# Gating branch of a hybrid decoder layer: the weight of v's norm applied behind the spatial sum, and three scalings moved between engines

## The chip, the cores and the metric

The kernel runs on one core of one Trainium2 chip. Its engines work side by side, each through its own queue in order: TensorE (PE, matrix products; PEld is its loading of weights), VectorE (DVE), ScalarE (ACT), GpSimd (POOL) and SyncE (SP, which issues the DMAs). The metric is the device time of one execution in microseconds. Instructions wait for each other by semaphores; an instruction that waits holds up everything behind it on its engine.

## The reference

One layer with two groups of heads. The input projection of the normalised input gives u, v and a gate zg for group A, and x, B, C, z and dt for group B (a chunked state-space scan, called SSD here). Group A is what the change touches:

```
def spatial_gating(u, v, zg, v_norm_w, v_norm_b, ws, bs, out_norm_w):
    vn = layer_norm(v, v_norm_w, v_norm_b).reshape(bsz, nc, CHUNK, GMLP_HEADS, GMLP_HEAD_DIM)
    ws_c = jnp.where(causal[None], ws, 0.0)
    s = jnp.einsum('hts,bcshd->bcthd', ws_c, vn) + bs.T[None, None, :, :, None]
    y = u * s * jax.nn.silu(zg)
    return grouped_rms_norm(y, out_norm_w, GMLP_HEAD_DIM)
```

Chunks have 128 positions, there are 8 heads of 128 channels, 2048 positions and a model width of 1024, all in float32. The spatial sum runs over positions t and s; v's norm has its mean and its root per position, its weight and bias per channel. Both groups' outputs go through one output projection, a norm and the residual sum.

## The kernel before

The 2048 positions are worked on as four blocks b of four chunks of 128 (NT = 4). The projections are large products on TensorE in seven units of 28 steps: six units u = 0 to 5 for the input projection (u = 3 gives v, u = 4 and 5 give u and zg of two head pairs each), u = 6 for the output projection. Each float32 operand is split into two parts (lines 160 and 161, on ScalarE and VectorE), and three products per pair accumulate in `acc` (lines 165 to 167). Blocks are combined in pairs by a scheme with seven products per unit (P1 to P7); `after` (lines 870 to 906) empties the accumulators and combines them, partly on ScalarE (line 876), partly on VectorE (lines 890 to 906).

Beside these products run small tasks, generators that are advanced between steps by `run_tasks`, each `yield d` asking for a pause of d time units. The tile scheduler then sets each engine's order at build time from its own model of costs, so an edit in one task can move instructions of others. The tasks are: the SSD stream (lines 344 to 540: convolution in lines 370 and 372, decay factors E in lines 389 and 394, operands xdt, xde in lines 434 to 438, the chunk's products y_ps and st_ps in lines 448 to 453, state in lines 457 and 458, outputs in lines 460 to 465), and for each block b and head pair hp (16 times) the gate:

- `spatial` (line 574) loads four chunks of v, 128 positions by 256 channels; VectorE subtracts the mean and multiplies by v's norm weight (line 584), ScalarE multiplies by the root r per position (line 585); TensorE forms the spatial sums s_ps (line 594); VectorE adds SB, which holds the biases (line 598).
- `gate_in` (line 608), called as each chunk of u and zg comes out of the projection: VectorE multiplies y by u (line 613), ScalarE forms silu(zg) (line 615), GpSimd multiplies the two (line 616), ScalarE sums the squares of each head (line 184).
- `gate_out` (line 622) computes the root g_r over those sums (VectorE line 171, GpSimd line 173, a power), ScalarE multiplies each half of each chunk by it (line 627, eight instructions), and `y_tiles` has TensorE transpose y (line 553) and ScalarE empty the result with the norm's weight (line 555).

PSUM, where TensorE writes, has five buffers for `acc` and three for all small products, so a late eviction holds up TensorE. Tiles of 256 channels (v, y, sg, xdt, xde and others) share 22 buffers, and operands of the products 7 (`r`), whose loads wait for a buffer.

Of the kernel before, what the change touches and what calls it, by code (L numbers as in the profile page):

```python
# [10 lines left out]
AF = mybir.ActivationFunctionType  # L11
ALU = mybir.AluOpType
# [3 lines left out]
P = 128  # L16
# [35 lines left out]
def hybrid_kernel(ctx: ExitStack, tc: tile.TileContext, x, x_t, pre_w, w_u, w_o, w_dt,  # L52
                  v_w, v_b, ws_t, bs_t, gn_w, conv_w, conv_b, dt_bias, a_log, d_skip, sn_w,
                  post_w, out):
    nc = tc.nc
# [12 lines left out]
    def bank(name):  # L68
        return ps.tile([P, T], F32, name=name, tag="ps")
# [7 lines left out]
    def qt(name):  # L77
        return qpool.tile([P, GC], F32, name=name, tag="q")
# [37 lines left out]
    SB = const.tile([P, 8, P], F32, name="SB")  # L116
# [24 lines left out]
    row_w = {}  # L141
# [27 lines left out]
    def rsqrt_mean(ss, n, inv, name):  # L169
        ms = sm.tile([P, n], F32, name=name + "_ms")  # L170
        nc.vector.tensor_scalar(ms, ss, inv, EPS, ALU.mult, ALU.add)  # L171
        r = sm.tile([P, n], F32, name=name + "_r")
        nc.gpsimd.tensor_tensor(r, ms, mhalf[:, 0:n], ALU.pow)  # L173
        return r
# [372 lines left out]
    def y_tiles(b, yg, j):  # L547
        for i in range(2):
            if i:
                yield 0  # L550
            tp = bank("y_tp")
            for c in range(NT):
                nc.tensor.transpose(out=tp[:, c * P:(c + 1) * P], in_=yg[c][:, i * P:(i + 1) * P], identity=ident)  # L553
            yT = gt("yT")
            nc.scalar.activation(yT, tp, AF.Copy, scale=y_c[:, 2 * j + i:2 * j + i + 1])
            store(y_d[b][j][:, i, :], yT, lambda i=i: y_in.add((b, j, i)))
# [17 lines left out]
    def spatial(b, hp):  # L574
        cols = slice(hp * GC, (hp + 1) * GC)
        mv, r = v_mv[b]
        v = []
        for c in range(NT):
            vc = qt("v")
            nc.sync.dma_start(out=vc, in_=v_d[b][c, :, cols])  # L580
            v.append(vc)
        yield 6
        for vc, c in zip(v, range(NT)):
            nc.vector.scalar_tensor_tensor(vc, vc, mv[:, c, 0:1], row_w["v"][:, cols], ALU.subtract, ALU.mult)
            nc.scalar.activation(vc, vc, AF.Copy, scale=r[:, c:c + 1])
        yield 8
        yg = []
        for half in range(2):
            sps = bank("s_ps")
            for cc in range(2):  # L590
                c = 2 * half + cc
                for i in range(2):
                    h = 2 * hp + i
                    nc.tensor.matmul(sps[:, cc * 256 + i * P:cc * 256 + (i + 1) * P], lhsT=wsT[:, h, :],  # L594
                                     rhs=v[c][:, i * P:(i + 1) * P], start=True, stop=True)
            for cc in range(2):
                y = qt("y")
                nc.vector.tensor_tensor(y, sps[:, cc * 256:(cc + 1) * 256],
                                        SB[:, 2 * hp:2 * hp + 2, :].rearrange("p h d -> p (h d)"), ALU.add)
                yg.append(y)  # L600
            if half == 0:
                yield 0
        gate[b, hp] = yg
# [4 lines left out]
    def gate_in(b, hp, c, t):  # L608
        if c == 0:
            run_out(spatial_task[b, hp])  # L610
            g_ss[b, hp] = sm.tile([P, NT, 2], F32, name="g_ss")
        y, ss = gate[b, hp][c], g_ss[b, hp]
        nc.vector.tensor_tensor(y, y, t[:, 0:GC], ALU.mult)
        sg = qt("sg")
        nc.scalar.activation(sg, t[:, GC:2 * GC], AF.Silu)
        nc.gpsimd.tensor_tensor(y, y, sg, ALU.mult)
        for i in range(2):
            sumsq(ss[:, c, i:i + 1], y[:, i * P:(i + 1) * P], P)
        if c == NT - 1:
            spawn(gate_out(b, hp), 4)  # L620

    def gate_out(b, hp):
        yg, ss = gate[b, hp], g_ss[b, hp]
        r = rsqrt_mean(ss[:, :, :].rearrange("p c i -> p (c i)"), NT * 2, 1.0 / P, "g")
        for c in range(NT):
            for i in range(2):
                nc.scalar.activation(yg[c][:, i * P:(i + 1) * P], yg[c][:, i * P:(i + 1) * P], AF.Copy,
                                     scale=r[:, 2 * c + i:2 * c + i + 1])
        yield 14
        yield from y_tiles(b, yg, hp)  # L630

# [290 lines left out]
    for group in groups:  # L922
        i = group[0]
        u, p, name, j = steps[i][:4]
# [9 lines left out]
        for uu in (4, 5):  # L934
            for b, n, w in WANTED:
                if i == uu * 28 + w - 5:
                    spatial_task[b, 2 * (uu - 4) + n] = spawn(spatial(b, 2 * (uu - 4) + n), 1)
# [69 lines left out]
```

## Time and profile before

| | |
|---|---|
| median of 3 timed runs | 1588.07 us (1584.94 to 1588.9) |
| the profiled execution | 1584.35 us |
| its span, first to last instruction | 1582.57 us |
| mean granted TensorE clock | 0.979 |
| busy: PE, DVE, ACT, POOL | 1508.9, 1068.9, 819.8, 390.1 us |

The profile's page gives the busy time of each engine; the windows give the same for chosen stretches with the granted clock of TensorE (1.00 is full speed); the timeline lists instructions in order with the idle time in front of each and what ended it. A busy TensorE at full clock can't be helped by other engines; idle time of another engine costs nothing by itself.

### The profile page before, as it was taken

To read this page: it belongs to the slowest core of one execution; us is meant where nothing else is said; L and a number is where in the kernel's file an instruction comes from. 1 tells how busy PE (TensorE), PEld (TensorE's weight loads), DVE (VectorE), ACT (ScalarE), POOL (GpSimd) and SP (SyncE) were. 2 spreads that over 40 slices of the span, in tenths; PEclk is the share of its full clock that TensorE was granted. 3 is DMA by queue.
4 is the path that set the end of the run, shared out by engine and by line. 5 is a ranking of instruction groups with operands and counts; after the bars stand their busy time and mean duration, and the time that the engine had idled before them with its cause. 6 is when DMAs were issued, how large, how long until landed. Compare 5 with 4: busy or idle time off the path is not lost.

```text
span 1582.6 us, 21521 instructions
## 1 busy us (share of the span) xinstructions
PE 1508.9 (95%) x7268; PEld 1258.4 (80%) x7268; DVE 1068.9 (68%) x1708; ACT 819.8 (52%) x1769; POOL 390.1 (25%) x449
## 2 busy tenths in 40 slices
PE   4979999899999999999999999989999999999996
PEld 3868887788888888888778888867888878888775
DVE  3476874678665576567786768764665646587698
ACT  4432324655676545654466666859737742333332
POOL 1000000234232333342234515353523300000022
PEclk9988999999999999999999999989999999999999
DMA  9799999999998799986998788866776598897998
GB/s 333 264 371 357 338 411 397 392 340 366 374 349 311 240 353 341 329 316 238 333 338 319 271 299 275 279 229 225 276 252 242 193 302 326 275 384 239 341 351 333
DMA packets 160847, 494.63 MB, mean 313 GB/s; under 512 B 19040, under 2 KB 35808, under 8 KB 140768
## 3 DMA queue, kind: packets, MB, share of 16 engines
q1 hardware_dynamic: 160736, 493.25, 85.9%
q8 instruction: 57, 0.93, 0.2%
q14 instruction: 54, 0.44, 0.1%
HBM read 373.51 MB, written 119.67 MB: 312 GB/s over the span
## 4 chain that ended last, share of the span: by engine, by line
PE 57%; DMA 13%; DVE 11%; ACT 7%; issue 3%; POOL 1%; SPq 1%; DVEq 0%; ACTq 0%; POOLq 0%
PE acc L165 16%; PE acc L167 16%; PE acc L166 16%; DMA E<-scr 3%; DMA r<-yd 3%; PE y_ps L448 3%; ACT E L389 2%; DMA r<-w_o 2%; PE y_ps L451 1%; PE st_ps L453 1%; DVE cv_out L372 1%; DVE a L161 1%; PE s_ps L594 1%; PE y_tp L553 1%; DVE b L161 1%
## 5 line engine op out<-in xcount | busy, mean ns | idle before, releaser
L165 PE MATMUL acc<-b,a 128*128 128x512 f32 x1344 | 544.6, 406 | 16.1 <-DMA a<-as0P 5.4
L166 PE MATMUL acc<-b,a 128*128 128x512 f32 x1344 | 527.3, 392 | 0.0
L167 PE MATMUL acc<-b,a 128*128 128x512 f32 x1344 | 520.2, 393 | 4.3 <-DVE a L161 4.3
L165 PEld LDWEIGHTS acc<-b,a 128*128 128x128 f32 x1344 | 253.7, 189 | 71.3 <-DMA a<-as0P 5.6
L167 PEld LDWEIGHTS acc<-b,a 128*128 128x128 f32 x1344 | 253.2, 188 | 60.2 <-DVE a L161 6.3
L166 PEld LDWEIGHTS acc<-b,a 128*128 128x128 f32 x1344 | 254.0, 189 | 49.3
L160 ACT ACTIVATE a<-r 128x1024 fp32r<-128x1024 f32 x96 | 101.1, 1057 | 200.8 <-PE acc L167 88.5
L165 PE MATMUL acc<-a,b 128*128 128x512 f32 x448 | 182.4, 414 | 8.3 <-ACT b L160 4.2
L372 DVE SCALAR_TENSOR_TENSOR cv_out<-cv_raw,cw,cv_out 128x512 f32<-128x512 f32 x192 | 155.1, 810 | 41.5 <-ACT cv_out L370 39.5
L161 DVE TENSOR_TENSOR b<-r,b 128x1024 fp32r<-128x1024 f32 x112 | 141.9, 1270 | 60.6 <-ACT b L160 60.4
L166 PE MATMUL acc<-a,b 128*128 128x512 f32 x448 | 180.3, 403 | 0.8 <-DVE a L161 0.8
L167 PE MATMUL acc<-a,b 128*128 128x512 f32 x448 | 177.7, 400 | 0.0
L160 ACT ACTIVATE b<-r 128x1024 fp32r<-128x1024 f32 x112 | 117.2, 1052 | 86.9 <-PE acc L167 33.1
L161 DVE TENSOR_TENSOR a<-r,a 128x1024 fp32r<-128x1024 f32 x96 | 117.3, 1223 | 50.5 <-ACT a L160 50.3
L165 PEld LDWEIGHTS acc<-a,b 128*128 128x128 f32 x448 | 87.2, 195 | 27.4 <-ACT b L160 4.3
L184 ACT ACTIVATE junk<-y 128x128 bf16<-128x128 f32 (+1 forms) x192 | 65.5, 341 | 83.1 <-POOL y L465 71.4
L457 POOL TENSOR_TENSOR state<-state,ex 128x256 f32<-128x256 f32 x60 | 46.9, 781 | 239.5 <-PE y_ps L451 239.4
L166 PEld LDWEIGHTS acc<-a,b 128*128 128x128 f32 x448 | 86.8, 194 | 19.6 <-DVE a L161 1.8
L167 PEld LDWEIGHTS acc<-a,b 128*128 128x128 f32 x448 | 86.4, 193 | 18.9 <-issue 0.2
L436 POOL TENSOR_TENSOR xde<-xtok,dte 128x256 f32<-128x256 f32 x64 | 52.3, 824 | 165.0 <-ACT xtok L408 158.7
L173 POOL TENSOR_TENSOR o_r<-o_ms,mhalf 128x1 f32<-128x1 f32 x16 | 19.0, 1198 | 295.1 <-DVE o_ms L171 285.0
L389 ACT ACTIVATE E<-E,cs 128x128 f32<-128x128 f32 x256 | 79.6, 390 | 22.2 <-DMA E<-scr 22.2
(163 smaller groups left out, 2125.8 us busy)
## 6 DMA issues: line engine op xcount, KB each, us to landing
a<-as0P SPq DMA_DIRECT2D x64, 1024.0 KB, 7.4
a<-as1P SPq DMA_DIRECT2D x64, 1024.0 KB, 6.2
r<-w_u SPq DMA_DIRECT2D x108, 512.0 KB, 6.4
r<-yd SPq DMA_DIRECT2D x72, 512.0 KB, 5.3
r<-hd SPq DMA_DIRECT2D x48, 512.0 KB, 7.5
r<-w_o SPq DMA_DIRECT2D x36, 512.0 KB, 5.2
E<-scr SPq DMA_DIRECT2D x64, 256.0 KB, 7.4
yd<-yT SPq DMA_DIRECT2D x64, 256.0 KB, 4.4
```

The lines of the kernel that those rows point to most:

```text
L160: nc.scalar.activation(w[:, :, 0, :], t, AF.Copy)
L161: nc.vector.tensor_tensor(w[:, :, 1, :], t, w[:, :, 0, :], ALU.subtract)
L165: nc.tensor.matmul(dst, lhsT=a_hi, rhs=b_hi, start=first, stop=False, skip_group_check=True)
L166: nc.tensor.matmul(dst, lhsT=a_hi, rhs=b_lo, start=False, stop=False, skip_group_check=True)
L167: return nc.tensor.matmul(dst, lhsT=a_lo, rhs=b_hi, start=False, stop=last, skip_group_check=True)
L173: nc.gpsimd.tensor_tensor(r, ms, mhalf[:, 0:n], ALU.pow)
L184: nc.scalar.activation(junk[:, 0:n], src, AF.Square, accum_out=dst)
L372: nc.vector.scalar_tensor_tensor(cv, raw[:, j:j + T], cw[:, ti, j:j + 1], cv, ALU.mult, ALU.add)
L389: nc.scalar.activation(E[:, h, :], E[:, h, :], AF.Relu, scale=-1.0, bias=dts[self.b]["cs"][:, o + h:o + h + 1])
L436: nc.gpsimd.tensor_tensor(h4(xde[:, :]), xc, hv(d["dte"], g, c), ALU.mult)
L448: nc.tensor.matmul(yps[:, h * HD:(h + 1) * HD], lhsT=E[:, h, :], rhs=xdt[:, h * HD:(h + 1) * HD], start=True, stop=True)
L457: nc.gpsimd.tensor_tensor(h4(st[:, :]), h4(st[:, :]), ev(d["ex"], 1, g, c), ALU.mult)
```

## The change

By linearity, the weight of v's norm, which is per channel, can be applied behind the sum over positions. So VectorE's line 584 becomes a scalar operation with two per-position operands (mean and root), and ScalarE's scaling of v goes. Behind the spatial sum VectorE multiplies by the weight (line 598, where SB was added), and GpSimd adds SB (line 599, new). In `gate_out`, ScalarE's eight scalings per gate become four products of 128x256 on GpSimd, with g_r broadcast along each head (line 627). Between lines 586 and 597, and from 628 on, the changed kernel's line numbers are one less than before.

```
@@ -581,8 +581,7 @@
         for vc, c in zip(v, range(NT)):
-            nc.vector.scalar_tensor_tensor(vc, vc, mv[:, c, 0:1], row_w["v"][:, cols], ALU.subtract, ALU.mult)
-            nc.scalar.activation(vc, vc, AF.Copy, scale=r[:, c:c + 1])
+            nc.vector.tensor_scalar(vc, vc, mv[:, c, 0:1], r[:, c:c + 1], ALU.subtract, ALU.mult)
@@ -595,8 +594,9 @@
             for cc in range(2):
                 y = qt("y")
-                nc.vector.tensor_tensor(y, sps[:, cc * 256:(cc + 1) * 256],
-                                        SB[:, 2 * hp:2 * hp + 2, :].rearrange("p h d -> p (h d)"), ALU.add)
+
+                nc.vector.tensor_tensor(y, sps[:, cc * 256:(cc + 1) * 256], row_w["v"][:, cols], ALU.mult)
+                nc.gpsimd.tensor_tensor(y, y, SB[:, 2 * hp:2 * hp + 2, :].rearrange("p h d -> p (h d)"), ALU.add)
                 yg.append(y)
@@ -623,9 +623,8 @@
         for c in range(NT):
-            for i in range(2):
-                nc.scalar.activation(yg[c][:, i * P:(i + 1) * P], yg[c][:, i * P:(i + 1) * P], AF.Copy,
-                                     scale=r[:, 2 * c + i:2 * c + i + 1])
+            y = yg[c][:, :].rearrange("p (i d) -> p i d", i=2)
+            nc.gpsimd.tensor_tensor(y, y, r[:, 2 * c:2 * c + 2].unsqueeze(2).broadcast_to([P, 2, P]), ALU.mult)
```

The scheduler orders the engines anew from the first gates on. Three places show it. The first is ScalarE early in unit 5, between two groups of line 876 (875 in the changed kernel), which empty accumulators; E, xtok and btok belong to the SSD stream, sg, v, y and yT to the gates. Before:

```order
L555 ACTIVATE yT<-y_tp,y_c 128x512
L184 ACTIVATE junk,g_ss<-y 128x128
L585 ACTIVATE v<-v,v_r_7296 128x256 x4
L394 ACT_TABLE_LOAD
L394 ACTIVATE E<-E 128x512
L408 ACTIVATE xtok<-xt_tp 128x512
L394 ACTIVATE E<-E 128x512 x2
L184 ACTIVATE junk,s_ss<-y 128x256
L555 ACTIVATE yT<-y_tp,y_c 128x512
L615 ACT_TABLE_LOAD
L615 ACTIVATE sg<-acc 128x256
L627 ACTIVATE y<-y,g_r 128x128 x8
```

and in the changed kernel:

```order
L555 ACTIVATE yT<-y_tp,y_c 128x512
L615 ACT_TABLE_LOAD
L615 ACTIVATE sg<-acc 128x256
L471 ACTIVATE y<-y,s_r 128x256 x4
L394 ACT_TABLE_LOAD
L394 ACTIVATE E<-E 128x512 x2
L408 ACTIVATE xtok<-xt_tp 128x512
L394 ACTIVATE E<-E 128x512
L555 ACTIVATE yT<-y_tp,y_c 128x512
L184 ACTIVATE junk,g_ss<-y 128x128
L615 ACT_TABLE_LOAD
L615 ACTIVATE sg<-acc 128x256 x2
```

The four scalings of v (line 585) and the eight of y (line 627) are gone; the loads of function tables stand as before.

The second place is VectorE at the end of unit 4 and the start of unit 5, some 20 us earlier. Lines 815 and 814 are the same subtraction on a weight operand, which waits for its load (r<-w_u); u_8272 and u_8264 are the same tile. Before:

```order
L463 TENSOR_TENSOR yo<-y_ps,ex_1125 128x256
L815 TENSOR_TENSOR r<-r 128x1024
L598 TENSOR_TENSOR y<-s_ps,SB 128x256
L613 TENSOR_TENSOR y<-y,u_8272 128x256
L598 TENSOR_TENSOR y<-s_ps,SB 128x256
L434 TENSOR_TENSOR xdt<-xtok,dt_577 128x256
L613 TENSOR_TENSOR y<-y,u_8287 128x256
L460 TENSOR_TENSOR y<-y_ps,xtok 128x256
L458 TENSOR_TENSOR state_243<-state_243,st_ps 128x256
L171 TENSOR_SCALAR g_ms<-g_ss 128x8
L463 TENSOR_TENSOR yo<-y_ps,ex_1125 128x256
L598 TENSOR_TENSOR y<-s_ps,SB 128x256 x2
```

and in the changed kernel:

```order
L818 TENSOR_TENSOR r<-r 128x1024
L598 TENSOR_TENSOR y<-s_ps,row_w 128x256 x2
L434 TENSOR_TENSOR xdt<-xtok,dt_577 128x256
L613 TENSOR_TENSOR y<-y,u_8264 128x256
L613 TENSOR_TENSOR y<-y,u_8279 128x256
L460 TENSOR_TENSOR y<-y_ps,xtok 128x256
L171 TENSOR_SCALAR g_ms<-g_ss 128x8
L458 TENSOR_TENSOR state_243<-state_243,st_ps 128x256
L814 TENSOR_TENSOR r<-r 128x1024
L372 SCALAR_TENSOR_TENSOR cv_out<-cv_raw,cw,cv_out 128x512 x3
L463 TENSOR_TENSOR yo<-y_ps,ex_1125 128x256
L598 TENSOR_TENSOR y<-s_ps,row_w 128x256 x2
```

The subtraction that waits for its load has moved behind two spatial sums, xdt, two gate products and the state; behind it now stand three convolution steps.

The third place is GpSimd in the same stretch, from the last gate products of one gate (line 616) on. Before:

```order
L616 TENSOR_TENSOR y<-y,sg 128x256 x4
L457 TENSOR_TENSOR state_243<-state_243,ex_1125 128x256
L436 TENSOR_TENSOR xde<-xtok,dte_1128 128x256
L438 TENSOR_TENSOR xtok<-xtok,hvec 128x256
L173 TENSOR_TENSOR g_r<-g_ms,mhalf 128x8
L464 TENSOR_TENSOR y<-y,yo 128x256
L465 TENSOR_TENSOR y<-y,zs 128x256
L457 TENSOR_TENSOR state_243<-state_243,ex_1125 128x256
L616 TENSOR_TENSOR y<-y,sg 128x256 x3
L436 TENSOR_TENSOR xde<-xtok,dte_1128 128x256
```

and in the changed kernel:

```order
L616 TENSOR_TENSOR y<-y,sg 128x256 x3
L599 TENSOR_TENSOR y<-y,SB 128x256 x2
L436 TENSOR_TENSOR xde<-xtok,dte_1128 128x256
L457 TENSOR_TENSOR state_243<-state_243,ex_1125 128x256
L438 TENSOR_TENSOR xtok<-xtok,hvec 128x256
L173 TENSOR_TENSOR g_r<-g_ms,mhalf 128x8
L627 TENSOR_TENSOR y<-y,g_r 128x256 x4
L464 TENSOR_TENSOR y<-y,yo 128x256
L599 TENSOR_TENSOR y<-y,SB 128x256
L465 TENSOR_TENSOR y<-y,zs 128x256
L599 TENSOR_TENSOR y<-y,SB 128x256
L457 TENSOR_TENSOR state_243<-state_243,ex_1125 128x256
```

Behind g_r there are now the four products of line 627, and the third and fourth addition of a gate (line 599) stand behind those.

## Rows read from the trace of the kernel before

**Rows 1.** The page: busy us, share of the span, instructions.
```profile
PE 1508.9 (95%) x7268; PEld 1258.4 (80%) x7268; DVE 1068.9 (68%) x1708; ACT 819.8 (52%) x1769; POOL 390.1 (25%) x449
```

**Rows 2.** Windows: length, busy us (instructions) by engine, clock, DMA.
```profile
800.00:1300.00 500.00, 485.43 (x2477) 408.37 (x2476) 330.02 (x585) 334.86 (x895) 189.11 (x210) 0.99 0.77 268
...
1040.00:1060.00 20.00, 13.97 (x70) 11.15 (x68) 12.16 (x25) 13.50 (x48) 15.05 (x18) 0.90 0.82 288
1060.00:1080.00 20.00, 18.46 (x86) 15.72 (x87) 8.73 (x22) 16.60 (x46) 5.92 (x9) 0.76 0.33 102
1080.00:1100.00 20.00, 17.48 (x91) 14.06 (x90) 7.05 (x13) 19.70 (x53) 8.92 (x9) 1.00 0.67 228
...
1200.00:1220.00 20.00, 20.00 (x107) 16.98 (x106) 11.72 (x23) 14.48 (x52) 6.71 (x8) 1.00 0.73 254
```

**Rows 3.** Windows of 2 us, the same columns.
```profile
1050.00:1052.00 2.00, 2.00 (x11) 1.79 (x9) 0.83 (x3) 0.96 (x4) 1.91 (x3) 0.50 0.99 391
...
1058.00:1060.00 2.00, 0.00 (x0) 0.00 (x0) 2.00 (x3) 2.00 (x6) 1.61 (x3) 0.84 0.31 117
...
1062.00:1064.00 2.00, 2.00 (x8) 1.82 (x8) 1.46 (x3) 1.23 (x5) 0.00 (x0) 0.50 0.33 122
```

**Rows 4.** Timeline: start, us, engine, line, [idle before, releaser].
```profile
1045.44 1.22 DVE L815 TENSOR_TENSOR r<-r 128x1024 f32<-128x1024 f32 x1 [4.26 <-DMA r<-w_u]
...
1047.94 0.63 PE L553 MATMUL y_tp<-ident,y 128*128 128x128 f32 x4 [1.67 <-DVE y L598]
...
1051.04 2.44 ACT L627 ACTIVATE y<-y,g_r 128x128 f32<-128x128 f32 x8 [3.72 <-POOL g_r L173]
...
1053.96 0.80 ACT L370 ACTIVATE cv_out<-cv_raw,cb,cw 128x512 f32<-128x512 f32 x1
...
1054.80 1.54 DVE L372 SCALAR_TENSOR_TENSOR cv_out<-cv_raw,cw,cv_out 128x512 f32<-128x512 f32 x2 [1.63 <-ACT cv_out L370]
...
1060.55 0.41 DVE L434 TENSOR_TENSOR xdt<-xtok,dt 128x256 f32<-128x256 f32 x1
...
1061.02 1.97 PE L448 MATMUL y_ps<-xdt,E 128*128 128x64 f32 x8 [4.32 <-DVE xdt L434]
```

**Rows 5.** Timeline at 1097 us.
```profile
1097.14 1.55 ACT L876 ACTIVATE p<-acc 128x512 f32<-128x512 f32 x3
...
1097.77 0.50 PE L165 MATMUL acc<-b,a 128*128 128x512 f32 x1 [2.48 <-ACT p L876]
```

**Rows 6.** Lines of ScalarE, 810:1285: busy us, mean ns, idle before.
```profile
L627 ACT ACTIVATE y<-y,g_r 128x128 f32<-128x128 f32 x128 | 39.2, 392 | 18.7 <-POOL g_r L173 18.7
...
L585 ACT ACTIVATE v<-v,v_r 128x256 f32<-128x256 f32 x64 | 30.0, 501 | 21.8 <-DVE v L584 21.4
```

**Rows 7.** The same lines, 1067:1097.2.
```profile
L627 ACT ACTIVATE y<-y,g_r 128x128 f32<-128x128 f32 x8 | 2.4, 390 | 0.0
...
L585 ACT ACTIVATE v<-v,v_r 128x256 f32<-128x256 f32 x4 | 1.7, 504 | 0.0
```

**Rows 8.** Single lines: duration ns min/median/max, first and last start.
```profile
L584 DVE SCALAR_TENSOR_TENSOR v<-v,v_mv,row_w x64: 468/479/1059, 815.6 to 1229.0; 128x256 f32<-128x256 f32 x64
...
L138 DVE TENSOR_SCALAR SB<-SB,rsum,bsT x8: 342/343/344, 210.0 to 211.8; 128x128 f32<-128x128 f32 x8
...
L598 DVE TENSOR_TENSOR y<-s_ps,SB x64: 405/414/425, 843.4 to 1247.7; 128x256 f32<-128x256 f32 x64
...
L613 DVE TENSOR_TENSOR y<-y,c x16: 409/436/950, 955.7 to 1200.9; 128x256 f32<-128x256 f32 x16
...
L464 POOL TENSOR_TENSOR y<-y,yo x60: 719/742/1977, 320.0 to 1191.5; 128x256 f32<-128x256 f32 x60
...
L457 POOL TENSOR_TENSOR state<-state,ex x60: 604/614/1594, 318.0 to 1191.0; 128x256 f32<-128x256 f32 x60
...
L173 POOL TENSOR_TENSOR g_r<-g_ms,mhalf x16: 1635/1637/2095, 874.5 to 1262.2; 128x8 f32<-128x8 f32 x16
```

**Rows 9.** Waits, 810:1285: total us, times, longest.
```profile
POOL y L616 <- ACT sg L615: 67.9, 17, 9.6
```

## The prediction, made before the changed kernel ran

> **What bounds the kernel now.** First the busy shares: TensorE is busy for 95% of the span and ScalarE for 52% [rows 1]. An average like this hides where the time can still move, so the stretches come next, and only the one that the change can reach: the spatial products and gates run from about 810 to 1270 us. In 1200:1220 TensorE is busy for all 20 us at full clock [rows 2]. There nothing that other engines do can shorten the time. Over 800:1300 TensorE is busy for 485.43 of 500 us [rows 2], so 14.57 us of idle time is the most that can go there, apart from the clock. Three neighbouring stretches hold most of it: 20 − 13.97 = 6.03, 20 − 18.46 = 1.54 and 20 − 17.48 = 2.52 us, together 10.09 us in 1040:1100 [rows 2]. The other 4.48 us I take as unchanged. In the same place the granted clock is 0.90 and 0.76 [rows 2], and the finer stretches show that it stands at 0.50 (1.2 instead of 2.4 GHz) around 1050 and again from 1060 on, after TensorE had stood still for all of 1058:1060 [rows 3]. 20 × 0.10 + 20 × 0.24 = 6.8 us is the upper bound of what that clock cost, since part of it fell into idle time.
>
> So there are two places. **The pile at 1045 to 1070**: VectorE stands 4.26 us before the weight operand of line 815, which a DMA brings at 1045.44. ScalarE stands 3.72 us before the eight scalings of line 627, because GpSimd still computes g_r, and so starts the convolution's first step (line 370) at 1053.96, for which VectorE waits 1.63 us. VectorE reaches xdt (line 434) at 1060.55, and TensorE has waited 4.32 us for it when it starts at 1061.02 [rows 4]. **The end at 1097.77**: TensorE waits 2.48 us for ScalarE to empty an accumulator (line 876) [rows 5]. ScalarE was busy for 19.70 of 20 us before [rows 2], and had not waited.
>
> **The change part by part.** No DMA and no matmul is added or taken away; three engines change.
>
> *ScalarE* loses 64 scalings of v (30.0 us) and 128 of y (39.2 us) [rows 6]. Nearly all of that lies beside a busy TensorE and is worth nothing. What counts is the run between two groups of line 876: in 1067 to 1097 four scalings of v (1.7 us) and eight of y (2.4 us) stand in the full ScalarE [rows 7], and the new order has neither between those groups. Line 876 then comes 4.1 us earlier against a wait of 2.48 us, so that wait goes: **−2.5 us**. What is late next there is the split of b (line 160) or TensorE's own y_tp, which ends just before. Bounds 0 and −2.5.
>
> *VectorE*: line 598 reads another constant and stays at 0.414 us. Line 584 becomes a scalar operation with two per-partition operands. The trace has no such operation at this size: the nearest row below is line 138, the same operation on half the elements (0.343), the nearest above the old line 584 (0.479) [rows 8]. I take the upper one, 0.48, since I need no gain from it; both ends differ by 64 × 0.14 = 9 us of VectorE's time, beside TensorE. What moves matters more. The order puts line 814 (the old 815, which waits for the DMA) behind two of line 598, xdt, two gate products, 460, g_ms and 458; these now run in the 4.26 us in which VectorE stood. From the start of the DMA-bound instruction to the xdt that held TensorE it took 1060.55 − 1045.44 = 15.1 us [rows 4]. In the new order there stand between the two: line 814 (1.22), six of line 372 at 1.54 / 2 = 0.77, two of 598 and one 458 and 463 at 0.42, two of 613 at 0.43, four of 584 at 0.48 [rows 4, 8]: 1.22 + 4.62 + 1.68 + 0.86 + 1.92 = 10.3 us. The wait for line 370 goes too, because its ScalarE queue no longer waits for g_r. Xdt comes 4.8 us earlier, less 0.3 us for the new wait below: **−4.5 us**. The DMA's landing I leave where it is. TensorE still stops here for several us, so I credit nothing for the clock. Bounds: 0, if the DMA lands later by what is gained, and −14.4 us, all idle time of 1040:1080 (7.57) and all of the clock (6.8).
>
> *GpSimd* gains 64 additions and 64 products with a broadcast operand. The nearest rows are line 464, two full operands, 0.742 us, and line 457, one of them broadcast, 0.614 us [rows 8]: 64 × 0.742 + 64 × 0.614 = 87 us on top of 189 in 500 [rows 2], 276, or 55%. As an engine it does not become the bound. But the additions stand inside a chain: VectorE's gate product (line 613) now waits for GpSimd's line 599, and whatever stands behind 613 on VectorE, evictions of accumulators and splits of b among them, waits with it, and TensorE for those. Mostly six to sixteen VectorE instructions stand between 598 and 613, 2.5 us or more at 0.42, which covers 0.742. In the pile it is two or three: about 0.3 us each for three pairs, the first already counted. Line 627 now stands on GpSimd behind g_r: four of 0.614 = 2.5 us, against 2.4 on ScalarE, ahead of transposes that are issued 14 time units later; that costs nothing while GpSimd is free.
>
> *Collisions.* Line 584 goes from 0.468 to 1.059 us and line 613 from 0.409 to 0.950, line 457 from 0.604 to 1.594 [rows 8], while the two engines run side by side. Between 0 and 0.54 us for each of 128 new operations is 0 to 69 us of VectorE's time, on 330 of 500 [rows 2]. At the upper end it is 80% busy and still beside TensorE, except where TensorE waits for VectorE. I take **+1.0 us** for collisions and the new wait together; 0 and +5 are the bounds, the upper from the 4.26 us that a VectorE standing still cost in the pile.
> The Trainium skill, SBUF — State Buffer, "Who interferes with whom", says that VectorE and GpSimd share a port pair as an exclusive lock, which a VectorE instruction takes with two SBUF inputs, or as a tensor_scalar in its two-port mode; the second one blocks fully. By it the new line 584 can still collide, as the old one could. The spreads above agree with a block of about a whole instruction. With one full block per new operation the +1.0 would be about +2, and the time 1583.
>
> The sum: −2.5 − 4.5 + 1.0 = −6.0 us on the profiled execution's own 1584.35 us (1582.57 of span and 1.78 around it) = 1578.3. The median of the timed runs, 1588.07, is 3.72 us above that execution, so the forecast in its terms is **1582 us**, with a range of its own of 1577 to 1587 us.
>
> **Rivals.**
> *The pile closes.* With g_r's wait gone from ScalarE and the DMA's wait filled, TensorE keeps its clock: 7.57 + 6.8 + 2.5 − 1.0 = 15.9 less about 1.5 for clock loss that was idle: 14.4 us, **1573.7 us**. For it: the 1.67 us that TensorE waits at 1047 hang on a line 598 that now comes before the DMA wait [rows 4]. Against: by my own count xdt still comes at about 1056, long after TensorE wants it. Chance 0.14.
> *Hidden.* The DMA-bound instruction only waits in another place, and behind it stand the convolutions and 463, so the pile moves as a whole. Then −2.5 + 1.0 = −1.5: **1586.6 us**. For it: TensorE's wait at 1061 is at the end of one queue that starts with a DMA. Chance 0.14.
> *GpSimd's queue becomes the wait* (the other side). In the pile the third addition (599) stands behind g_r (1.637), four of line 627 (2.46) and one 464 (0.742): with its own 0.742 that is 5.6 us from g_ms [rows 8]. It decides from the point at which VectorE needs less than 5.6 us from g_ms to its third gate product; my count of what lies there (0.42 + 1.22 + 2.3 + 0.42 + 0.8 = 5.2 us) is close to that. GpSimd also stands in order before late ScalarE results, 67.9 us in 17 waits, up to 9.6 us [rows 9], and additions now queue behind these. One stop of VectorE of 5.6 us that reaches TensorE where it had none, with a clock loss of the size seen here (I take 5.5 us of the 6.8), against the 2.5 won: +8.6, **1596.7 us**. Against: the order interleaves the additions, and most pairs are far apart. Chance 0.24.
>
> **How the numbers follow.** The forecast has a chance of 0.48. About 0.3%, or 4.8 us, is what a measurement here tells from no change: 1583.3 and 1592.8 are the limits. Two thirds of the forecast lie under 1583.3 (0.32), the rest (0.16) is no change. Faster: 0.32 + 0.14 = 0.46; no change: 0.16 + 0.14 = 0.30; slower: 0.24. The range of 8 in 10 reaches from the better part of the closing pile to the middle of the slow case: 1572 to 1596 us.
>
> **What would show it.** Right: TensorE's wait for line 875 (the old 876) near 1095 is gone; ScalarE's busy time falls by about 69 us and GpSimd's rises by 87 to 110; the wait of y_ps for xdt ends some 4 to 5 us earlier; 1200:1220 is still full. Wrong: VectorE's line 613 waits for GpSimd's 599 by several us at a time and TensorE behind it; a stretch of half clock outside 1050 to 1070; or the old wait of 4.3 us is still there at full length.

## The result and the profile after

The changed kernel took 1597.34 us (median of 20 runs, 1589.7 to 1603.69), the kernel before 1587.9 us (20 runs beside it). The ratio on record is 1.0053 with a 95% interval of 1.0038 to 1.0067 (the two medians alone would give 1.0059): slower, by more than the 0.3% that can be told apart. The forecast of 1582 us had the wrong sign, and 1597.34 lies 1.3 us outside the range of 8 in 10 (1572 to 1596 us). The rival of GpSimd's queue had given 1596.7 us.

The span of the profiled execution grew from 1582.6 to 1593.1 us. The busy shares on the page of the changed kernel, which answer to [rows 1]:

```profile
PE 1506.3 (95%) x7268; PEld 1254.3 (79%) x7268; DVE 1089.3 (68%) x1708; ACT 759.0 (48%) x1577; POOL 492.2 (31%) x577
```

ScalarE has 61 us less and GpSimd 102 us more, close to the forecast (69 less, 87 to 110 more). VectorE has 20 us more with the same number of instructions. The windows, with the columns of [rows 2]:

```profile
800.00:1300.00 500.00, 474.95 (x2431) 397.47 (x2430) 344.83 (x580) 270.54 (x700) 290.48 (x339) 0.99 0.76 260
...
980.00:1000.00 20.00, 19.15 (x92) 15.89 (x92) 16.68 (x30) 14.24 (x46) 12.84 (x14) 0.91 0.73 246
...
1040.00:1060.00 20.00, 16.14 (x87) 12.81 (x85) 15.35 (x25) 7.95 (x26) 18.48 (x21) 1.00 0.77 282
1060.00:1080.00 20.00, 10.92 (x53) 9.48 (x54) 11.48 (x22) 10.79 (x38) 14.37 (x19) 0.74 0.39 134
1080.00:1100.00 20.00, 16.95 (x87) 13.44 (x86) 8.22 (x14) 18.33 (x46) 8.01 (x11) 1.00 0.52 179
1200.00:1220.00 20.00, 20.00 (x102) 17.05 (x102) 14.40 (x26) 8.90 (x30) 17.96 (x22) 1.00 0.60 216
```

In 800:1300 TensorE is idle for 25.05 us, before for 14.57 [rows 2]. The difference of 10.5 us is as large as the difference of the spans (1593.1 − 1582.6), and the two executions part here: the first spatial sum (line 598) starts 0.5 us later than before (843.9 against 843.4), the last one 11.4 us later (1259.1 against 1247.7; [rows 8] and the last section). 1200:1220 is still full. Of the 10.5 us, 5.4 lie in 1040:1080 (12.94 us idle instead of 7.57), where GpSimd is busy for 18.48 and 14.37 of 20 us, and 0.5 in 1080:1100. The remaining 4.6 us (9.06 idle instead of 4.48) are in stops of under 2 us each between 860 and 1160 us. Behind one of them the granted clock falls far from the pile, to 0.91 over 980:1000; that was one of the prediction's signs of being wrong. The timeline of the pile, in the columns of [rows 4]:

```profile
1044.89 1.75 DVE L818 TENSOR_TENSOR r<-r 128x1024 f32<-128x1024 f32 x1
1048.63 0.43 DVE L598 TENSOR_TENSOR y<-s_ps,row_w 128x256 f32<-128x256 f32 x1 [2.00 <-POOL y L616]
...
1052.83 0.24 DVE L171 TENSOR_SCALAR g_ms<-g_ss 128x8 f32<-128x8 f32 x1
...
1053.41 1.28 DVE L814 TENSOR_TENSOR r<-r 128x1024 f32<-128x1024 f32 x1
...
1053.58 2.62 POOL L173 TENSOR_TENSOR g_r<-g_ms,mhalf 128x8 f32<-128x8 f32 x1
1056.28 2.84 POOL L627 TENSOR_TENSOR y<-y,g_r 128x256 f32<-128x256 f32 x4
1059.08 0.72 POOL L464 TENSOR_TENSOR y<-y,yo 128x256 f32<-128x256 f32 x1
1059.77 0.72 POOL L599 TENSOR_TENSOR y<-y,SB 128x256 f32<-128x256 f32 x1
...
1060.52 0.93 DVE L613 TENSOR_TENSOR y<-y,u 128x256 f32<-128x256 f32 x1 [2.58 <-POOL y L599]
...
1067.79 0.41 DVE L434 TENSOR_TENSOR xdt<-xtok,dt 128x256 f32<-128x256 f32 x1
1068.35 1.94 PE L448 MATMUL y_ps<-xdt,E 128*128 128x64 f32 x8 [8.56 <-DVE xdt L434]
1071.54 0.99 PE L165 MATMUL acc<-b,a 128*128 128x512 f32 x1
...
1061.15 0.47 SPq L735 DMA_DIRECT2D a<-as1P  x1
```

Read it from the bottom up. TensorE stands 8.56 us for xdt, where it stood 4.32 before [rows 4]. VectorE comes to xdt 14.4 us after line 814 (1067.79 − 1053.41), not 10.3. In between, its gate product (line 613) waits 2.58 us for the addition (line 599), and the addition stands behind g_r, four products of line 627 and one line 464. Line 814 no longer waits for its DMA, but only because it starts at 1053.41 instead of 1045.44: ahead of it VectorE has waited for GpSimd again, for a buffer that line 616 frees (2.00 us).

The last row (SPq is the queue that issues SyncE's DMAs) shows a second wait that ends at almost the same moment. The accumulation at 1071.54 needs operand a, whose load (a<-as1P) is issued at 1061.15 and lands at 1067.96. Before, the same load was issued at 1047.08, right behind the load of w_u; now it stands behind the load of w_u that waits for line 814 (issued at 1054.72) and behind the loads of v, one of which waits 2.6 us for GpSimd's line 464 to free a buffer. So an earlier xdt alone would have let that accumulation start at 1067.96 at the earliest, 3.6 us sooner than it did.

The stop near 1097 us [rows 5] has changed. TensorE's two waits there in the changed kernel:

```profile
1094.04 1.16 PE L422 MATMUL cb_ps<-cv_out 128*128 128x128 f32 x8 [2.21 <-ACT xtok L408]
...
1097.12 0.50 PE L165 MATMUL acc<-b,a 128*128 128x512 f32 x1 [0.80 <-ACT sg L615]
...
PE acc L165 <- ACT p L875: 2.4, 2, 1.6
```

The wait for line 876 (now 875) is gone there, but others of ScalarE stand in its place: 1080:1100 has 3.05 us of idle time, before 2.52. Elsewhere it has come up anew: the last row has TensorE's waits for line 875 in 800:1300 (total us, times, longest), 1.63 us at 874 us and 0.74 at 1076, together 2.4 us, about as much as the one wait before.

### The profile page after: what moved, and what is told of

Its sections match the earlier page's. It is cut to its first block, busy times and chain, and to the rows that moved or that the text cites. A ratio compares the mean times of both kernels' runs of the same rounds, so it can differ in the third digit from the quotient of the medians.

```text
span 1593.1 us, 21479 instructions
## 1 busy us (share of the span) xinstructions
PE 1506.3 (95%) x7268; PEld 1254.3 (79%) x7268; DVE 1089.3 (68%) x1708; ACT 759.0 (48%) x1577; POOL 492.2 (31%) x577
## 4 chain that ended last, share of the span: by engine, by line
PE 58%; DMA 13%; DVE 11%; ACT 6%; issue 3%; POOL 1%; SPq 0%; DVEq 0%; ACTq 0%; POOLq 0%
PE acc L165 16%; PE acc L167 16%; PE acc L166 16%; DMA E<-scr 3%; PE y_ps L448 3%; DMA r<-yd 3%; DMA r<-w_o 2%; ACT E L389 2%; DVE a L161 2%; PE y_ps L451 1%; PE st_ps L453 1%; DVE cv_out L372 1%; DVE b L161 1%; PE y_tp L553 1%; PE s_ps L593 1%
## 5 line engine op out<-in xcount | busy, mean ns | idle before, releaser
L165 PE MATMUL acc<-a,b 128*128 128x512 f32 x448 | 182.1, 413 | 10.5 <-ACT b L160 4.7
L372 DVE SCALAR_TENSOR_TENSOR cv_out<-cv_raw,cw,cv_out 128x512 f32<-128x512 f32 x192 | 159.8, 835 | 35.8 <-ACT cv_out L370 33.0
L161 DVE TENSOR_TENSOR b<-r,b 128x1024 fp32r<-128x1024 f32 x112 | 145.1, 1298 | 49.4 <-ACT b L160 49.3
L376 ACT ACTIVATE cv_out<-cv_out 128x512 f32<-128x512 f32 x64 | 40.3, 630 | 109.5 <-DVE cv_out L372 109.1
```

The costliest lines, as they stand in the source:

```text
L161: nc.vector.tensor_tensor(w[:, :, 1, :], t, w[:, :, 0, :], ALU.subtract)
L165: nc.tensor.matmul(dst, lhsT=a_hi, rhs=b_hi, start=first, stop=False, skip_group_check=True)
L372: nc.vector.scalar_tensor_tensor(cv, raw[:, j:j + T], cw[:, ti, j:j + 1], cv, ALU.mult, ALU.add)
L376: nc.scalar.activation(self.cv[i], self.cv[i], AF.Silu)
```

## The experiments

All ratios are to the kernel before, with 95% intervals. My first theory after the result was the **block theory**: an addition that stands behind g_r and the four products of line 627 in GpSimd's queue stops VectorE's gate product. Its rivals were the chain (the addition alone), the load with its collisions, the buffers that GpSimd frees late, and the order of the instructions itself.

### Halves of the change

The scaling of y back on ScalarE (x1_y_act), and both that and the addition of SB on VectorE (x4_no_pool). Short diffs against the changed kernel:

```
-            y = yg[c][:, :].rearrange("p (i d) -> p i d", i=2)
-            nc.gpsimd.tensor_tensor(y, y, r[...].broadcast_to([P, 2, P]), ALU.mult)
+            for i in range(2):
+                nc.scalar.activation(yg[c][:, i * P:(i + 1) * P], ..., AF.Copy, scale=r[...])
x4_no_pool, also:
-                nc.gpsimd.tensor_tensor(y, y, SB[...], ALU.add)
+                nc.vector.tensor_tensor(y, y, SB[...], ALU.add)
```

> The changed kernel with the scaling of y (line 627) back on ScalarE; only the addition of SB stays on GpSimd. GpSimd then has some 46 us more than before instead of 102. Queue theory (GpSimd's queue is full in the dense stretch, mostly by the block of four products behind g_r): most of the 10 us goes, time 1588 to 1591 us (ratio to before 1.000 to 1.002), VectorE's wait for line 599 near 1060 under 1 us. Chain theory (the addition on GpSimd between lines 598 and 613 costs, wherever it stands): the loss stays, 1595 to 1599 (1.005). Chance order (any reordering of this place moves the time by this much): no forecast, anything from 1580 to 1600.

> The changed kernel with nothing added to GpSimd: the addition of SB on VectorE, the scaling of y on ScalarE; left of the change are line 584 with both scalars and the 64 scalings less on ScalarE (30 us), for 26 us more on VectorE. Queue theory and chain theory: both causes are gone, 1583 to 1588 (ratio 0.997 to 1.000). If VectorE itself is what the pile waits for (its own work, not GpSimd), 26 us more there show as a longer wait for xdt: 1592 or more.

x2_add_dve makes only the second edit; x3_y_pool_only puts line 627's new form into the kernel before and nothing else.

> The changed kernel with the addition of SB on VectorE behind line 598; the scaling of y stays on GpSimd as one product per chunk. VectorE gets 64 x 0.41 = 26 us more, GpSimd 50 us less. Queue theory: the four products behind g_r still block GpSimd, so that lines 464 and 616 and the buffers they free come late; half of the loss or more stays, 1592 to 1596 (ratio 1.002 to 1.005). Chain theory: the loss goes, 1584 to 1589.

> The kernel before with one edit, the scaling of y on GpSimd as one product per chunk (64 products instead of 128 scalings on ScalarE). Queue theory: this edit alone loses, 1592 to 1597 us (ratio 1.003 to 1.006), TensorE's wait for xdt grows. Chain theory: no addition in the chain, so no loss: 1583 to 1588 (0.997 to 1.000).

Measured: x1 1.0012 (0.9994 to 1.0030), x2 0.9992 (0.9975 to 1.0009), x3 0.9980 (0.9962 to 0.9998), x4 1.0000 (0.9985 to 1.0015). None has the loss of 0.5%. The chain theory, by which x1 should have kept it, fails; the queue theory in its first form, by which x2 and x3 should have kept half, fails too. VectorE as the bound fails with x2 and x4: x2 has VectorE busy for 361.92 us of 800:1300, more than the changed kernel (344.83), and loses nothing. So far only the two GpSimd parts together lose; the last part of this section tries that at other settings.

x2 also shows the second wait of the pile by itself. Its timeline:

```profile
1052.34 1.21 DVE L814 TENSOR_TENSOR r<-r 128x1024 f32<-128x1024 f32 x1
...
1045.76 0.39 SPq L735 DMA_DIRECT2D a<-as0P  x1
1053.58 0.33 SPq L153 DMA_DIRECT2D r<-w_u  x1
...
1055.83 0.38 SPq L735 DMA_DIRECT2D a<-as1P  x1
...
1063.41 0.79 PE L165 MATMUL acc<-b,a 128*128 128x512 f32 x1 [6.35 <-DMA a<-as1P]
1063.75 0.94 DVE L434 TENSOR_TENSOR xdt<-xtok,dt 128x256 f32<-128x256 f32 x1
1066.14 1.80 PE L448 MATMUL y_ps<-xdt,E 128*128 128x64 f32 x8
```

Here the xdt of the pile starts at 1063.75, 4.0 us earlier than in the changed kernel and 3.2 us later than before [rows 4], and TensorE doesn't wait for it. Yet 1040:1080 has 8.89 us of idle time (before 7.57, changed 12.94): TensorE first waits 6.35 us for its operand a. That DMA is issued at 1055.83, because SyncE's queue stood from 1045.76 to 1053.58 before the load of w_u, which went out when line 814 had ended. So beside the wait for xdt there is a second one, in SyncE's queue, that an earlier xdt alone doesn't remove.

### Block, buffers, load

The block cut in two with 13 units behind it (y1_split_block), ScalarE for the sixth and seventh gate alone (y2_two_gates), 25 buffers (y3_q25), and the load without the chain on the kernel before (y4_idle_load):

```
y1:          for c in range(NT):
+                if c == 2:
+                    yield 1
...
-        yield 14
+        yield 13
y2:  for gates 6 and 7 of 16 the ScalarE loop of x1
y3:  -  qpool ... bufs=22        +  qpool ... bufs=25
y4:  (before) +  nc.gpsimd.tensor_tensor(idle, SB[0:2], SB[2:4], ALU.add)   # behind 598, and 4 per gate
```

> The changed kernel with the block of four products of line 627 cut in two: one time unit between the second and the third, and 13 in place of 14 behind them, so that an addition (line 599), line 464 or line 616 can stand between. GpSimd's work is the same. Block theory (an addition that stands behind g_r and four products in GpSimd's queue stops VectorE's gate product, and neither does so alone): half of the loss or more goes, 1588 to 1593 us (ratio 1.001 to 1.003). Load theory (the sum of GpSimd's work and its collisions with VectorE costs, in whatever order): the loss stays, 1595 to 1599 (1.005).

> The changed kernel with the scaling of y back on ScalarE for two of the sixteen gates only, the sixth and the seventh, which are those of the pile at 1036 and 1056 us; GpSimd loses 8 products of 64 (5 us of its 102 more). Block theory: the 5.4 us more that TensorE stands in 1040 to 1080 go, 1590 to 1593 us (ratio 1.002 to 1.003). Load theory: a twentieth of the load goes, so 1596 to 1597 (1.005).

> The changed kernel with 25 buffers of the size of a gate's chunk instead of 22; no operation changes its engine. Buffer theory (VectorE's line 598 and ScalarE's silu wait for GpSimd only because it frees their buffers late, 6.0 us in six and 15.0 us in three waits): half of the loss or more goes, 1589 to 1593 us (ratio 1.001 to 1.003). Block theory, by the chain from 599 to 613: the loss stays, 1594 to 1598.

> The kernel before with 128 additions put on GpSimd at the places of the new ones (64 behind line 598, four in each gate behind g_r), which read a constant and write a tile that nobody reads: the same load, queue and collisions, without the chain from 598 over 599 to 613, and with ScalarE as full as before. Load theory: 1594 us or more (ratio 1.004 or more). Block theory: the chain is missing, so at most late buffers: 1587 to 1591 (1.000 to 1.002).

Measured: y1 1.0001 (0.9985 to 1.0018), y2 1.0011 (1.0000 to 1.0022), y3 1.0056 (1.0037 to 1.0076), y4 1.0212 (1.0191 to 1.0234). y1 has GpSimd as full as the changed kernel (289.45 us of 800:1300) and loses nothing, against the load theory; y2 puts an eighth of the products back and loses a fifth as much. By their times both fit the block theory. But the waits don't. In y2 the 5.4 us in 1040:1080 should have gone; TensorE is idle there for 10.81 us, only 2.1 less than in the changed kernel, and most of what y2 wins lies behind 1080. The load of a is issued as late there (1062.00) as in the changed kernel; y1 issues it at 1050.66. VectorE's waits for GpSimd in 800:1300 (total us, times, longest) of y1:

```profile
DVE state L458 <- POOL state L457: 9.4, 6, 2.8
DVE y L613 <- POOL y L599: 8.9, 7, 3.8
DVE y L598 <- POOL y L616: 2.2, 3, 1.3
```

of y2, TensorE's longest:

```profile
PE y_ps L448 <- DVE xdt L434: 6.5, 1, 6.5
```

and of y3, with TensorE's longest below:

```profile
DVE state L458 <- POOL state L457: 11.1, 9, 1.8
DVE y L598 <- POOL y L616: 0.3, 1, 0.3
...
PE acc L165 <- ACT sg L615: 5.2, 3, 2.5
PE y_ps L451 <- DVE state L458: 4.6, 3, 2.4
PE y_tp L553 <- ACT xtok L408: 4.4, 1, 4.4
```

y1 waits 8.9 us for the addition and loses nothing. y3 never waits for it, its waits for buffers are all but gone, and it loses 0.56%, in other places. So neither that wait nor late buffers can be the cause by themselves, and the block theory as one named stop has fallen.

y4 missed its aim. Its additions need no operand of the dense stretch, and all were run early:

```profile
210.17 3.23 POOL L601 TENSOR_TENSOR idle<-SB 128x256 f32<-128x256 f32 x4 [52.30 <-DVE SB L138]
...
341.69 6.33 POOL L631 TENSOR_TENSOR idle<-SB 128x256 f32<-128x256 f32 x8
...
PE y_ps L451 <- DVE state L458: 21.4, 1, 21.4
```

From 210 to 348 us they fill GpSimd; TensorE then waits 21.4 us for a state that comes behind them. It says nothing of the dense stretch, so the load without the chain remains untested there, but it shows that work which no one waits for costs 2% where it stands in front of work that someone does.

### The order itself

If the places of the loss change with each edit, the order of the instructions may be the cause. The number of time units between the scaling of y and its transposes (14) shifts the order and changes no operation:

```
-        yield 14
+        yield 13   (z1 changed kernel, z3 before)    15 (z2, z4)    16 (w1, v4)
```

> The changed kernel with 13 time units in place of 14 between the scaling of y and its transposes; the block of four stays whole and every operation stays on its engine. Block theory (an addition behind g_r and four products): the loss stays, 1593 to 1599 us (ratio 1.004 to 1.007). Order theory (the operations' engines cost nothing by themselves; the changed kernel has a bad order in the dense stretch, and any small shift gives another): the loss goes for the most part, 1584 to 1591 (0.998 to 1.002).

> The same with 15 in place of 14. Block theory: 1593 to 1599 us (ratio 1.004 to 1.007). Order theory: a draw of its own, most likely 1584 to 1592 (0.998 to 1.003), and not the same as with 13.

> The kernel before with 13 time units in place of 14, nothing else: what a shift of the order alone is worth where GpSimd has no more work. Block theory: within 0.2% of before, 1584 to 1591 us. Order theory: it can lose as the changed kernel did, 1582 to 1597 (0.997 to 1.006).

> The kernel before with 15 time units in place of 14, nothing else. Block theory: 1584 to 1591 us. Order theory: 1582 to 1597 (0.997 to 1.006), not the same as with 13.

> The kernel before with 16 time units in place of 14. At 13, 14 and 15 it has 1.0027, 1 and 0.9958. Trend theory (the later the transposes are issued, the less TensorE's queue waits at them): 0.992 to 0.995, 1574 to 1579 us. Order theory: no trend, 0.997 to 1.004.

> The changed kernel with 16 time units in place of 14. The kernel before at 16 has 0.9950; the change lost 0.37, 0.53 and 0.41% against it at 13, 14 and 15. Pair theory: 0.998 to 1.001, 1584 to 1588 us. Order theory (three draws that happened to agree): no offset, 0.993 to 0.997.

The halves once more at other settings (v1 and w2 are x1 with 15 and 16 units, v2 is x2 with 15, v3 is x3 with 15):

> The changed kernel with the scaling of y on ScalarE (as in the earlier run of that edit) and 15 time units in place of 14. The kernel before at 15 has 0.9958, the changed one at 15 has 0.9999. Pair theory (the loss of 0.4% that the change has at 13, 14 and 15 units needs both the addition and the block on GpSimd): 0.995 to 0.998, 1579 to 1583 us. Addition theory (the addition alone carries it, and its 1.0012 at 14 was a lucky order): 0.999 to 1.001, 1585 to 1588. Order theory (no operation carries it, each order is a draw of its own): anything from 0.995 to 1.005.

> The changed kernel with the addition of SB on VectorE and 15 time units in place of 14. Pair theory: 0.994 to 0.997, 1577 to 1582 us, as at 14 it lay 0.1% under the kernel before. Block theory (the four products alone carry the loss, and the 0.9992 at 14 was a lucky order): 0.999 to 1.001. Order theory: anything from 0.995 to 1.005.

> The kernel before with only the scaling of y on GpSimd and 15 time units in place of 14. If its gain at 14 (0.2%) and that of the fifteenth unit (0.4%) are causes of their own and add up: 0.994, 1577 us, faster than every kernel so far. If both come out of the same waits in the pile: 0.995 to 0.997. Order theory: anything from 0.995 to 1.005.

> The changed kernel with the scaling of y on ScalarE and 16 time units in place of 14: the part of the change that cost nothing at 14 and 15, at the setting that was best for the kernel before. Pair theory: no offset against the kernel before at 16, 0.994 to 0.996, 1577 to 1581 us, as fast as the fastest so far. Addition theory: 0.998 to 1.000.

| units | before | changed | y on ScalarE (x1) | addition on VectorE (x2) | y on GpSimd alone (x3) |
|---|---|---|---|---|---|
| 13 | 1.0027 (1.0012 to 1.0042) | 1.0064 (1.0042 to 1.0086) | | | |
| 14 | 1 | 1.0053 (1.0038 to 1.0067) | 1.0012 | 0.9992 | 0.9980 |
| 15 | 0.9958 (0.9939 to 0.9976) | 0.9999 (0.9983 to 1.0014) | 0.9959 (0.9945 to 0.9974) | 0.9970 (0.9954 to 0.9987) | 0.9994 (0.9976 to 1.0011) |
| 16 | 0.9950 (0.9932 to 0.9968) | 1.0053 (1.0030 to 1.0075) | 0.9990 (0.9974 to 1.0007) | | |

No theory met all of its forecasts. The block theory held with 13 units (z1) and failed with 15 (z2), and it failed for the kernel before, which moved by more than its 0.2% (z3, z4). The order theory held for z2 and z3 and missed z1; it gave z4 and v4 too little gain and w1 no loss. v4 lies on the edge of the trend theory. The pair theory held for v1 and v2 and failed for w1 (above its range) and w2, which lies where the addition theory had it; v3 lies outside both of its first two forecasts.

Two things follow. One unit moves either kernel by up to 0.5%, with no operation added. There is no trend that both share: before falls to 16, the changed kernel rises again. And the changed kernel loses against the kernel before at each of the four settings: 0.37, 0.53, 0.41 and 1.03% (the two kernels with 16 units ran on two chips, each beside the kernel before). The halves lie between −0.20 and +0.40% of it (+0.12, +0.01, +0.40, −0.08, +0.12, −0.20, +0.36; mean 0.10). The kernel before by itself spans 0.77% over the four settings, so one difference of 0.4% may be a draw: the +0.40 of w2, the +0.36 of v3, and y1's recovery too. Four losses of about 0.4% or more in the same direction are hardly draws, but that is an argument from four pairs, and nothing shows it beyond them. That it takes both GpSimd parts is not shown either, as w2 and v3 make one of them each and lose about as much as the whole change does at 13 or 15 units.

What is the same in the four pairs stands in the profiles. I add up the rows of the waits in 800:1300 for which VectorE waited for GpSimd, and those for which TensorE waited for VectorE, and take VectorE's busy time from the windows:

| units | VectorE waits for GpSimd, us | VectorE busy, us | TensorE waits for VectorE, us |
|---|---|---|---|
| 13 | 12.9 to 22.1 | 325.33 to 339.24 | 9.6 to 13.3 |
| 14 | 9.4 to 19.9 | 330.02 to 344.83 | 10.3 to 17.8 |
| 15 | 13.1 to 23.4 | 333.18 to 350.36 | 6.6 to 10.5 |
| 16 | 18.4 to 29.6 | 332.43 to 340.95 | 8.8 to 14.3 |

(each from before to changed). VectorE waits 9.2 to 11.2 us longer for GpSimd and is busy 8.5 to 17.2 us longer, and TensorE waits 3.7 to 7.5 us longer for VectorE, at every setting. The six halves that make one of the GpSimd moves at 14 and 15 have 7.1 to 11.6 us in the last column, inside or near the range of before.

These sums go with the change; they don't set the time. y1 has VectorE waiting for GpSimd for 23.7 us and busy for 344.75, about as much as the changed kernel or more, and loses nothing. y3 has 11.4 us of such waits and 8.7 us in the last column, less than before has there, and loses 0.56%: its TensorE waits for ScalarE instead, 13.4 us where before has 4.2. And the kernel before with 16 units, the fastest of all, waits nearly as long for GpSimd (18.4 us) as the changed kernel with 14 (19.9). Nor does the late load of a set it alone: the changed kernel with 16 units issues it at 1049.50 and loses the most. So the common cause of the four losses stays open.

Where the delay comes out differs by setting. Three of TensorE's waits in the changed kernel at 16 units:

```profile
PE y_tp L553 <- DVE state L458: 5.5, 2, 3.2
...
PE y_tp L553 <- DVE y L598: 2.9, 2, 2.1
...
PE y_ps L448 <- DVE xdt L434: 0.9, 1, 0.9
```

xdt, which held the pile at 14 units for 8.6 us, has 0.9 us here; line 458 waits for GpSimd's line 457, and line 598 for buffers, in its place.

The faster version came out of the control: the kernel before with 15 or 16 units (0.9958 and 0.9950, some 1581 and 1580 us) beats both kernels, with x1 at 15 beside them (0.9959). In the profile of before with 15 units, whose execution of 1572.49 us was the fastest of its 12 and 8 us under their median, the stretch after the stop is full and at full clock (columns of [rows 2]):

```profile
1040.00:1060.00 20.00, 14.77 (x83) 11.96 (x82) 14.40 (x29) 14.34 (x43) 14.31 (x17) 1.00 0.72 259
1060.00:1080.00 20.00, 20.00 (x112) 17.08 (x111) 8.55 (x22) 17.71 (x56) 11.24 (x14) 1.00 0.60 211
```

TensorE loses 5.23 us here, before 7.57 with clocks of 0.90 and 0.76 [rows 2].

## Why the prediction was wrong

TensorE's idle time in 800:1300 grew by 10.5 us where the sum said −6.0. By the prediction's places: +0.5 at the stop of line 876, +5.4 in the pile, and +4.6 in the stretches whose 4.48 us it took as unchanged.

**ScalarE, −2.5 us.** The wait named is gone from its place, but the term was mis-sized: ScalarE's xtok and sg stand there instead (2.21 and 0.80 us), so the stretch lost 0.5 us, and line 875 holds TensorE up for 2.4 us elsewhere. I had named the split of b as what is late next, not other work of ScalarE; an engine that had been full for 19.70 of 20 us is still full for 18.33.

**The pile, −4.5 us.** This step failed first, and by most: +5.4 us. It said that two of line 598, xdt and the products would run "in the 4.26 us in which VectorE stood". That gap was gone before they could start. VectorE ended line 463 2.6 us later than before, and a split of b (line 161) and line 818 (1.25 and 1.75 us), which had run earlier before, came in between; line 818 ended at 1046.64, already 1.2 us after 1045.44, the start of the DMA-bound instruction before. Then VectorE waited 2.00 us for GpSimd, and the instructions themselves took 4.8 us (1048.63 to 1053.41, with two more waits of 0.26 for GpSimd). So line 814 began 8.0 us later than I had it. And the 10.3 us from there to xdt were 14.4: the 2.58 us wait, 1.0 us more in two of line 613 (0.93 and 0.94 for 0.43 each), 0.9 more in six of line 372 and 0.6 more in four of line 584, less some 0.9 by which neighbours overlap in the profile. Even a right count would not have given 4.5 us, as the late load of a shows in the changed kernel and in x2: I had looked at VectorE's queue and not at SyncE's.

**GpSimd, +1.0 us for collisions and the new wait, bounds 0 and +5.** This term was too small. It was sized from the additions' place in one queue, where "most pairs are far apart"; what the runs show is 9 to 11 us more of waiting in VectorE at every setting, spread over buffers, states and gate products, and 8 to 17 us more of busy time. In the pile alone the new waits are 2.00 us for a buffer and 2.58 us for the addition. How much of all this reaches TensorE at other places is not shown, as y1 has as much of both and loses nothing.

**The 4.48 us taken as unchanged** became 9.06. The prediction gave no reason for leaving these stretches out, although the order changes from the first gates on.

**The rival.** I gave GpSimd's queue 0.24, with a deciding point: VectorE needs less than 5.6 us from g_ms to its third gate product. It needed 5.1 (from 1052.83 to 1057.94, where the wait begins; I had counted 5.2), and GpSimd 7.7 (to 1060.52), since g_r took 2.62 us instead of 1.64 and the four products 2.84 instead of 2.46. By my own count the point was crossed; I should have given that case the most. That its time came within 1 us is luck: the stop of VectorE was 2.58 us and not 5.6; the clock cost, reckoned as in the prediction, 7.0 us (0.74 over 1060:1080 and 0.91 over 980:1000) against 6.8 before, and not 5.5 more; and the 2.5 us at line 876 were not won. One stop of VectorE is at most part of the loss: y3 loses as much without that wait.

**What I did not count at all** is the order. One time unit is worth up to 0.5%, more than the −6.0 us that I forecast. No forecast of 0.4% for an edit that reorders the program could be surer than that.

**Still open:** the cause of the loss. Which of the waits carries it at a given setting can't be told from one profile each, what the four pairs have in common is not found beyond the sums above, and whether cutting the block (y1) is a cure or a good draw was not tried at a second setting.

## What to carry to other kernels

Before work is moved to an engine with idle time, look at what stands in its queue where the program is dense, and who waits for what it hands back: results and free buffers. GpSimd was busy for 25% of the span and still late in a stretch where it had 15 of 20 us. A change of half a per cent in a program with a background schedule should be timed at two or three neighbouring settings of that schedule, for both kernels: here the four pairs pointed the same way, and the settings alone held a gain that the change had not. And when an instruction that frees a buffer moves, look at SyncE's queue too: the loads behind the one that waits for that buffer move with it.

## What the runs showed of the hardware

Which VectorE instructions are stretched beside a busy GpSimd depends on where their operands lie. The single lines of the changed kernel (duration in ns, min/median/max, first and last start):

```profile
L598 DVE TENSOR_TENSOR y<-s_ps,row_w x64: 406/415/427, 843.9 to 1259.1; 128x256 f32<-128x256 f32 x64
...
L613 DVE TENSOR_TENSOR y<-y,acc x16: 407/411/423, 854.4 to 1129.2; 128x256 f32<-128x256 f32 x16
L613 DVE TENSOR_TENSOR y<-y,u x16: 410/708/959, 1011.8 to 1268.8; 128x256 f32<-128x256 f32 x16
...
L584 DVE TENSOR_SCALAR v<-v,v_mv,v_r x64: 399/414/962, 816.3 to 1240.4; 128x256 f32<-128x256 f32 x64
...
L599 POOL TENSOR_TENSOR y<-y,SB x64: 716/742/1722, 844.4 to 1260.1; 128x256 f32<-128x256 f32 x64
L627 POOL TENSOR_TENSOR y<-y,g_r x64: 607/616/1596, 875.9 to 1277.0; 128x256 f32<-128x256 f32 x64
```

The same line 613 never takes over 0.423 us when one operand is an accumulator in PSUM, and has a median of 0.708 when both lie in SBUF. The Trainium skill, SBUF — State Buffer, "Who interferes with whom", says that a VectorE instruction with at most one SBUF input does not contend with GpSimd, outside the two-port modes; these rows agree. Line 598, with s_ps in PSUM, has a GpSimd instruction beside it in 54 of its 64 cases and never takes over 0.427. Line 584, with one SBUF tile and two per-partition operands, has a median of 0.414 us, but a maximum of 0.962, so it does collide: the 31 of its 64 cases without a GpSimd instruction beside them take 0.399 to 0.417 us, the 33 others have a median of 0.698. Whether it runs in a two-port mode no row names. An estimate of its price per column: from line 138, the same operation on 128x128 (0.343 [rows 8]), to these 128x256 it is 0.071 us for 128 columns, about half of what the old form takes per column (0.273 us for 256, from the old line 584 with 0.479 to line 372 on 128x512 with 0.752, both in the kernel before). The new GpSimd operations had the medians that the nearest rows gave (0.742 and 0.616 for 0.742 and 0.614).
